# The recurrent mixer's (1 + t)/(1 − t) rewritten with an exponential on ScalarE, silu by Tanh, and a gate buffer with one place for odd and one for even blocks

## The chip, the cores and the metric

The kernel runs on one core of one Trainium2 chip. The metric is the time of one execution on the device in microseconds. A core has a matrix engine (TensorE, PE in the profile), an elementwise engine (VectorE, DVE), an engine for functions by table (ScalarE, ACT), a general engine (GpSimd, POOL), and a queue engine that here issues nearly all DMAs (SyncE, SP). Each runs its own instructions in the order in which they were written for it, and waits for others through semaphores. Matrix products are collected in PSUM, eight banks of 512 float32 columns by 128 partitions.

## The reference, cut to what matters

One decoder layer on x of 1024 tokens by 1024 features: a norm, one wide projection, an attention mixer (compressed, selected and window branches) and a recurrent mixer, each with a silu gate, merged and projected out. The recurrent mixer, which the change rewrites, is

```
uc = conv_b + sum(up[:, k:k + S] * conv_w[k] for k in range(4))
r = sigmoid(uc @ lru_wa + lru_ba);  i = sigmoid(uc @ lru_wx + lru_bx)     # block diagonal
log_a = -8 * r * softplus(-lru_lambda)
a = exp(log_a);  b = sqrt(-expm1(2 * log_a)) * (i * uc)
h[s] = a[s] * h[s - 1] + b[s]
y_b = (h * silu(g_lru)) @ w_proj_b
```

and the compression of keys and values is silu(flat @ w1 + b1) @ w2, whose key part is then normalised by its mean square.

## The kernel before

Float32 products are made of three products of split operands: mm3 (L169 to L172) issues hi·hi, lo·hi and hi·lo, so every product is a group of three matmuls. The hi part of a tile is written by ACT and the lo part by a subtraction on DVE or POOL.

The stage that the change touches is the first quarter of the program, up to some 250 us of it. The recurrent mixer works on 512 channels as four blocks of 128 channels by all 1024 tokens. `lru(n)` is a generator in two parts: first two chunks of the input projection (the convolution's input and the gate g_lru), the convolution and the silu gate; then two gate products of 128x1024 (the gates r and i, into PSUM banks named ps_t, of which there are two), the recurrence's coefficients, and the scan. `compress()` is a generator too. A string sets in which order their parts are written:

```
ORD = "0c1c0c2c1c323"
```

Behind it `qkv` projects all eight token blocks with matmuls of 262 columns into banks ps_s and ps_f; each finished block is copied out by ACT (L510, L511) and twelve gate columns by DVE (L512, bg). `prep` (L533 to L580) then normalises the block's queries and keys in steps that are handed out between other work: ACT squares (L543), DVE sums (L545), POOL takes the root (L192, L193), DVE multiplies (L548), POOL applies the gains (L549, L550), ACT and DVE split into hi and lo (L553 to L558, and POOL L562 for the values), PE transposes (L566, L573) into ps_t, ACT and DVE cast these (L568, L577). The attention's scores begin at L624.

The coefficients before: with t = tanh(half the log of a) the kernel uses a = (1 + t)/(1 − t), and sqrt(1 − a²) = 2 sqrt(−t)/(1 − t). ACT makes t (L368) and sqrt(−t) (L369); DVE 1 − t (L373), its reciprocal (L374), the two products (L375, L376); POOL i·uc (L377), DVE its product with the root (L378), the scan (L379), POOL the product with the gate (L380).

A scheduler places the instructions of each engine in order of a priority that counts up as the program is written; `urgent(by)` lowers it by so much for what is written inside. The kernel has a ring of nine tiles t of 128x1024, and one tile kTs, which here holds the silu gate in its first half and the gate i in its second.

Of the kernel before, what the change touches and what calls it, by code (L numbers as in the profile page):

```python
# [9 lines left out]
FT = mybir.dt.float32  # L10
FR = mybir.dt.float32r
AF = mybir.ActivationFunctionType
# [5 lines left out]
S = 1024  # L18
# [3 lines left out]
HD = 64  # L22
# [48 lines left out]
F_LEAD = 3.13  # L71


def f(ap):
    return ap.bitcast(FT)
# [11 lines left out]
def _build(ctx, tc, A, out, dbg):  # L87
# [217 lines left out]
    with tc.issue_after(last_c), tc.issue_after(last_v):  # L305
        C.activation(gw_h, gw_raw, AF.Copy)
        V.tensor_tensor(out=gw_l, in0=gw_raw, in1=f(gw_h), op=OP.subtract)
        cb1 = part["cb1"].rearrange("p (j h) -> p j h", j=2)
        pe = part["pe"].rearrange("p (j l) -> p j l", j=2)
# [18 lines left out]
        V.tensor_scalar(out=m4sp, in0=y[:, 5], scalar1=-8.0, scalar2=None, op0=OP.mult)  # L328


    yb = DR.tile([4, 128, S], FT, name="yb")

    def lru(n):
# [17 lines left out]
        si = K.tile([128, 2, 64 + S], FT, name="kTs", bufs=1)  # L351
        sg, i = si[:, 0, :S], si[:, 1, :S]
        for half in range(2):
            t = slice(half * 512, (half + 1) * 512)
            C.activation(sg[:, t], s[half], AF.Sigmoid)
            V.tensor_tensor(out=sg[:, t], in0=sg[:, t], in1=s[half], op=OP.mult)
        yield
        r = u
        for w, b_, g_ in ((0, ba, r), (1, bx, i)):
            for half in range(2):  # L360
# [3 lines left out]
                C.activation(g_[:, t], s, AF.Sigmoid, bias=b_[:, n:n + 1])  # L364
        sc = m4sp[:, n:n + 1]

        a, q = ta(), ta()
        C.activation(a, r, AF.Tanh, scale=sc)  # L368
        C.activation(q, a, AF.Sqrt, scale=-1.0)  # L369
        if LE == 2:  # L370
            C.activation(r, a, AF.Copy, scale=-1.0, bias=1.0)
        else:
            EN[LE].tensor_scalar(out=r, in0=a, scalar1=-1.0, scalar2=1.0, op0=OP.mult, op1=OP.add)  # L373
        V.reciprocal(r, r)  # L374
        V.scalar_tensor_tensor(out=a, in0=a, scalar=1.0, in1=r, op0=OP.add, op1=OP.mult)  # L375
        V.scalar_tensor_tensor(out=q, in0=q, scalar=2.0, in1=r, op0=OP.mult, op1=OP.mult)  # L376
        EN[IE].tensor_tensor(out=i, in0=i, in1=uc, op=OP.mult)  # L377
# [7 lines left out]
    def compress():  # L385
# [7 lines left out]
        for j in range(2):  # L393
# [29 lines left out]
            for hf in range(2):  # L423
                z = s[hf][:, 0:128]
                C.activation(sg[:, hf], z, AF.Sigmoid, bias=cb1[:, j, hf:hf + 1])
                V.scalar_tensor_tensor(out=hid[:, hf], in0=z, scalar=cb1[:, j, hf:hf + 1], in1=sg[:, hf],
                                       op0=OP.add, op1=OP.mult)
# [6 lines left out]
            if j == 0:  # L434
# [4 lines left out]
                rsq(ss, ss, HD * EPS, 64, 2)  # L439
# [12 lines left out]
            else:  # L452
                for r in (slice(0, 64), slice(64, 128)):
                    C.activation(vcc[r, :, 0], ov, AF.Copy)
# [664 lines left out]
```

## Time and profile before

| | |
|---|---|
| median of three runs | 905.2 us (902.38 to 905.53) |
| the profiled execution | 903.51 us, span of the trace 901.7 us |
| mean granted clock of TensorE | 0.996 |
| busy share | PE 97%, DVE 63%, ACT 49%, POOL 33% |
| the chain of work that ended last | PE 83%, DVE 6%, POOL 3%, DMA 3%, ACT 3% of the span |

The trace shows one execution. Busy time is the time in which an engine executes, as a share of the span; the chain that ended last is followed back from the last instruction, at each step to what released it. Matmuls are pipelined: one that lasts 0.39 us can be followed by the next 0.23 us after its start, so starts are compared, not durations. A wait is the idle time of an engine just before an instruction, put down to the instruction that released it.

### The profile page before, as it was taken

Reading aid. Unit: us, or ns where it says so; the run is one execution under the profiler, and the core shown is the slowest. Engines: PE = TensorE matmul, PEld = TensorE weight load, DVE = VectorE, ACT = ScalarE, POOL = GpSimd, SP = SyncE. Lnnn points to the kernel's source line nnn. Section 1 sums busy time; section 2 is a strip of 40 time slices with the busy share of each in tenths; the row PEclk is TensorE's granted clock in tenths of the full one; section 3 lists DMA queues with packets and bytes.
Section 4 is the critical chain, followed back from the end, with each engine's and each line's share of the span. In section 5 each row is a group of like instructions: output and inputs, shape, how many; then the busy total and the mean of one; then the engine's idle time right before and its main releaser. Section 6 shows DMA issues by size and latency. Waiting matters only on the chain.

```text
span 901.7 us, 15836 instructions
## 1 busy us (share of the span) xinstructions
PE 872.1 (97%) x5670; PEld 779.5 (86%) x5670; DVE 569.1 (63%) x1627; ACT 441.4 (49%) x1161; POOL 298.5 (33%) x338
## 2 busy tenths in 40 slices
PE   5999999989899999999999999999999999999998
PEld 4778888989899999999999998999998877888887
DVE  4563868897622548576577857667777886783111
ACT  7432453646423547566456757566667663331000
POOL 4032243279512435253355644233324421000000
PEclk9999999999999999999999999999999999999999
DMA  9133421202212112112122241121113369883121
GB/s 354 53 99 114 155 87 48 77 30 76 101 48 83 47 60 84 64 53 77 48 65 77 67 138 54 37 71 56 40 46 117 125 212 342 330 271 109 71 71 47
DMA packets 45519, 92.49 MB, mean 103 GB/s; under 512 B 6896, under 2 KB 12704, under 8 KB 45440
## 3 DMA queue, kind: packets, MB, share of 16 engines
q1 hardware_dynamic: 44480, 88.33, 29.3%
q0 software_dynamic: 960, 3.15, 0.9%
q8 instruction: 44, 0.72, 0.3%
q14 instruction: 35, 0.29, 0.1%
HBM read 64.15 MB, written 25.21 MB: 99 GB/s over the span
## 4 chain that ended last, share of the span: by engine, by line
PE 83%; DVE 6%; POOL 3%; DMA 3%; ACT 3%; issue 1%; SPq 0%; ACTq 0%; DVEq 0%; POOLq 0%
PE ps_f L170 10%; PE ps_f L171 9%; PE ps_f L172 9%; PE ps_s L624 7%; PE ps_s L170 7%; PE ps_s L172 7%; PE ps_s L171 7%; PE ps_t L677 6%; PE ps_t L170 4%; PE ps_t L171 4%; PE ps_t L172 4%; PE ps_o L701 3%; PE ps_o L702 3%; DVE sq L548 1%; POOL ss L193 1%
## 5 line engine op out<-in xcount | busy, mean ns | idle before, releaser
L171 PE MATMUL ps_f<-big_l,w_hi 128*128 128x256 f32 (+1 forms) x700 | 200.3, 286 | 0.0
L170 PE MATMUL ps_f<-big_h,w_hi 128*128 128x256 f32 (+1 forms) x664 | 193.8, 292 | 0.8 <-ACT ev L841 0.6
L172 PE MATMUL ps_f<-big_h,w_lo 128*128 128x256 f32 (+1 forms) x664 | 189.6, 286 | 0.0
L171 PEld LDWEIGHTS ps_f<-big_l,w_hi 128*128 128x128 f32 x700 | 131.9, 188 | 2.0
L170 PEld LDWEIGHTS ps_f<-big_h,w_hi 128*128 128x128 f32 x664 | 125.6, 189 | 4.5 <-ACT ev L841 2.0
L172 PEld LDWEIGHTS ps_f<-big_h,w_lo 128*128 128x128 f32 x664 | 125.4, 189 | 1.8 <-POOL w_lo L185 0.3
L682 DVE TENSOR_TENSOR pl<-ps_t,ph 128x512 fp32r<-128x512 f32 x132 | 90.4, 687 | 47.1 <-ACT ph L681 45.6
L185 POOL TENSOR_TENSOR w_lo<-w_raw,w_hi 128x1024 fp32r<-128x1024 f32 x32 | 77.9, 2438 | 97.6 <-ACT w_hi L184 75.0
L681 ACT ACTIVATE ph<-ps_t 128x512 fp32r<-128x512 f32 x132 | 78.1, 599 | 48.8 <-PE ps_t L677 45.5
L662 POOL TENSOR_SCALAR p_slc<-p_slc,mx,bg 128x384 f32<-128x384 f32 (+7 forms) x88 | 68.6, 785 | 90.1 <-DVE mx L661 35.3
L658 ACT ACTIVATE p_slc<-ps_s,mx 128x256 f32<-128x256 f32 (+5 forms) x128 | 68.1, 540 | 24.0 <-DVE mx L656 18.2
L171 PE MATMUL ps_s<-big_l,w_hi 128*128 128x512 f32 (+1 forms) x184 | 73.2, 398 | 0.0
L184 ACT ACTIVATE w_hi<-w_raw 128x1024 fp32r<-128x1024 f32 (+1 forms) x40 | 42.3, 1061 | 38.3 <-PE ps_f L171 17.7
L648 DVE TENSOR_REDUCE mx<-ps_s 128x1 f32<-128x256 f32 (+5 forms) x120 | 50.9, 436 | 10.7 <-PE ps_s L624 9.2
L701 PE MATMUL ps_o<-ph,t 128*128 128x512 f32 x132 | 55.7, 422 | 0.0
L170 PE MATMUL ps_s<-big_h,w_hi 128*128 128x512 f32 x136 | 54.4, 408 | 0.4 <-ACT big_h L245 0.3
L662 POOL TENSOR_SCALAR p_win<-p_win,mx,bg 128x640 f32<-128x640 f32 (+1 forms) x40 | 34.7, 869 | 59.1 <-DVE mx L661 25.0
L677 PE MATMUL ps_t<-ident_r,p_slc 128*128 128x128 f32 x336 | 54.0, 273 | 0.0
L653 DVE CUSTOM_DVE_ANT_0 ps_s<-ps_s,bias 128x256 f32<-128x256 f32 (+1 forms) x128 | 52.5, 417 | 2.3 <-POOL p_win L662 0.8
L172 PE MATMUL ps_s<-big_h,w_lo 128*128 128x512 f32 x136 | 53.4, 395 | 0.4 <-POOL w_lo L185 0.4
L624 PE MATMUL ps_s<-kTs,t 128*128 128x512 f32 (+4 forms) x224 | 53.0, 349 | 0.3 <-ACT pc L633 0.3
L702 PE MATMUL ps_o<-pl,t 128*128 128x512 f32 x132 | 53.2, 403 | 0.0
(332 smaller groups left out, 2209.9 us busy)
## 6 DMA issues: line engine op xcount, KB each, us to landing
w_raw<-in_w_in SPq DMA_DIRECT2D x30, 512.0 KB
t<-in_x SPq DMA_DIRECT2D x8, 512.0 KB
gb<-ev SPq DMA_DIRECT2D x16, 256.0 KB
ga<-ev SPq DMA_DIRECT2D x16, 256.0 KB
w_raw<-in_w_out SPq DMA_DIRECT2D x8, 512.0 KB
st<-mb SPq DMA_DIRECT2D x16, 256.0 KB
w_raw<-in_w_tok SPq DMA_DIRECT2D x6, 524.0 KB
ev<-in_cw SPq DMA_DIRECT2D x8, 256.0 KB
```

The lines of the kernel that those rows point to most:

```text
L170: T.matmul(o, lh, rh, start=first, stop=False)
L171: T.matmul(o, lh, rl, start=False, stop=False)
L172: T.matmul(o, ll, rh, start=False, stop=last)
L185: (E or (V if tail else G)).tensor_tensor(out=lo, in0=raw, in1=f(hi), op=OP.subtract)
L624: T.matmul(s, qT[h][:, i * 128:(i + 1) * 128], rhs, start=(hl == 0), stop=(hl == 1))
L658: C.activation(p[:, h, k0:k1], sv, AF.Exp, bias=mx[:, 6:7], accum_out=mx[:, 7 + j:8 + j])
L662: G.tensor_scalar(out=p[:, h], in0=p[:, h], scalar1=mx[:, 9:10], scalar2=bg[:, g, i, 4 * (br + 1) + h:4 * (br + 1) + h + 1], op0=OP.mult, ...
L677: ins = T.transpose(pt[:, h * 128:(h + 1) * 128], p[h][:, c0:c0 + 128], ident)
L681: C.activation(ph, pt, AF.Copy)
L682: V.tensor_tensor(out=pl, in0=pt, in1=f(ph), op=OP.subtract)
L701: T.matmul(o, vf, pp[0], start=first, stop=False)
L702: T.matmul(o, vf, pp[1], start=False, stop=False)
```

## The change

Algebra: with a = (1 + t)/(1 − t), 1/(1 − t) is (1 + a)/2. So `r` becomes a by an exponential on ACT (L378 of the changed kernel, with a new column of scales m8sp, twice m4sp), and the two factors are made from it: q = (1 + a)·½sqrt(−t), and a again as (1 + a)·t + 1, which is the old formula written out. The half in q is made good by a gate of twice the silu: (tanh(z/2) + 1)·z. The compression's silu is written in the same way; its keys are normalised with 4 eps, its values halved in the copy out of PSUM. That silu is written under urgent(600). The gate i is computed ahead of r, into a tile of the ring of its own, and the tile kTs is taken once, with one half for the gate of even blocks and one for that of odd blocks. The product i·uc (POOL) is written ahead of the coefficients. The diff:

```diff
--- before.py
+++ after.py
@@ -69,6 +69,7 @@
 F_PREP = 1.24
 F_JOB = 1.16
 F_LEAD = 3.13
+UH = 600
 
 
 def f(ap):
@@ -306,6 +307,8 @@
         C.activation(gw_h, gw_raw, AF.Copy)
         V.tensor_tensor(out=gw_l, in0=gw_raw, in1=f(gw_h), op=OP.subtract)
         cb1 = part["cb1"].rearrange("p (j h) -> p j h", j=2)
+        cb1h = K.tile([128, 2, 2], FT, name="cb1h")
+        V.tensor_scalar(out=cb1h, in0=cb1, scalar1=0.5, scalar2=None, op0=OP.mult)
         pe = part["pe"].rearrange("p (j l) -> p j l", j=2)
 
 
@@ -326,9 +329,13 @@
         V.tensor_tensor(out=y[:, 5], in0=y[:, 5], in1=y[:, 6], op=OP.add)
         m4sp = K.tile([128, 4], FT, name="m4sp")
         V.tensor_scalar(out=m4sp, in0=y[:, 5], scalar1=-8.0, scalar2=None, op0=OP.mult)
+        m8sp = K.tile([128, 4], FT, name="m8sp")
+        V.tensor_scalar(out=m8sp, in0=m4sp, scalar1=2.0, scalar2=None, op0=OP.mult)
 
 
     yb = DR.tile([4, 128, S], FT, name="yb")
+
+    si = K.tile([128, 2, 64 + S], FT, name="kTs", bufs=1)
 
     def lru(n):
         s = chunk(2 * n)
@@ -348,33 +355,31 @@
         C.activation(uh, uc, AF.Copy)
         EN[UE >> n & 1].tensor_tensor(out=ul, in0=uc, in1=f(uh), op=OP.subtract)
         s = chunk(2 * n + 1)
-        si = K.tile([128, 2, 64 + S], FT, name="kTs", bufs=1)
-        sg, i = si[:, 0, :S], si[:, 1, :S]
+        sg, i = si[:, n % 2, :S], ta()
         for half in range(2):
             t = slice(half * 512, (half + 1) * 512)
-            C.activation(sg[:, t], s[half], AF.Sigmoid)
-            V.tensor_tensor(out=sg[:, t], in0=sg[:, t], in1=s[half], op=OP.mult)
+
+            C.activation(sg[:, t], s[half], AF.Tanh, scale=0.5)
+            V.scalar_tensor_tensor(out=sg[:, t], in0=sg[:, t], scalar=1.0, in1=s[half], op0=OP.add, op1=OP.mult)
         yield
         r = u
-        for w, b_, g_ in ((0, ba, r), (1, bx, i)):
+        for w, b_, g_ in ((1, bx, i), (0, ba, r)):
             for half in range(2):
                 s = ps_t()
                 t = slice(half * 512, (half + 1) * 512)
                 mm3(s, gw_h[:, w, n], gw_l[:, w, n], uh[:, t], ul[:, t], True, True)
                 C.activation(g_[:, t], s, AF.Sigmoid, bias=b_[:, n:n + 1])
+        EN[IE].tensor_tensor(out=i, in0=i, in1=uc, op=OP.mult)
         sc = m4sp[:, n:n + 1]
+
 
         a, q = ta(), ta()
         C.activation(a, r, AF.Tanh, scale=sc)
-        C.activation(q, a, AF.Sqrt, scale=-1.0)
-        if LE == 2:
-            C.activation(r, a, AF.Copy, scale=-1.0, bias=1.0)
-        else:
-            EN[LE].tensor_scalar(out=r, in0=a, scalar1=-1.0, scalar2=1.0, op0=OP.mult, op1=OP.add)
-        V.reciprocal(r, r)
-        V.scalar_tensor_tensor(out=a, in0=a, scalar=1.0, in1=r, op0=OP.add, op1=OP.mult)
-        V.scalar_tensor_tensor(out=q, in0=q, scalar=2.0, in1=r, op0=OP.mult, op1=OP.mult)
-        EN[IE].tensor_tensor(out=i, in0=i, in1=uc, op=OP.mult)
+        C.activation(r, r, AF.Exp, scale=m8sp[:, n:n + 1])
+        C.activation(q, a, AF.Sqrt, scale=-0.25)
+        V.scalar_tensor_tensor(out=q, in0=r, scalar=1.0, in1=q, op0=OP.add, op1=OP.mult)
+        V.scalar_tensor_tensor(out=a, in0=r, scalar=1.0, in1=a, op0=OP.add, op1=OP.mult)
+        EN[LE].tensor_scalar(out=a, in0=a, scalar1=1.0, scalar2=None, op0=OP.add)
         EN[JE >> n & 1].tensor_tensor(out=i, in0=i, in1=q, op=OP.mult)
         V.tensor_tensor_scan(out=q, data0=a, data1=i, initial=0.0, op0=OP.mult, op1=OP.add)
         EN[YE >> n & 1].tensor_tensor(out=q, in0=q, in1=sg, op=OP.mult)
@@ -422,9 +427,12 @@
             hid, sg = [hs[:, o:o + 256].rearrange("p (h c) -> p h c", h=2) for o in (0, 256)]
             for hf in range(2):
                 z = s[hf][:, 0:128]
-                C.activation(sg[:, hf], z, AF.Sigmoid, bias=cb1[:, j, hf:hf + 1])
-                V.scalar_tensor_tensor(out=hid[:, hf], in0=z, scalar=cb1[:, j, hf:hf + 1], in1=sg[:, hf],
-                                       op0=OP.add, op1=OP.mult)
+
+                with urgent(UH):
+                    C.activation(sg[:, hf], z, AF.Tanh, scale=0.5, bias=cb1h[:, j, hf:hf + 1])
+                    V.tensor_scalar(out=hid[:, hf], in0=z, scalar1=cb1[:, j, hf:hf + 1], scalar2=None, op0=OP.add)
+                    V.scalar_tensor_tensor(out=hid[:, hf], in0=sg[:, hf], scalar=1.0, in1=hid[:, hf],
+                                           op0=OP.add, op1=OP.mult)
             o = ps_t()
             for g in range(2):
                 for hf in range(2):
@@ -436,7 +444,7 @@
                 ss = hs[0:64, 640:642]
                 for g in range(2):
                     C.activation(kq[:, g], ov[:, g], AF.Square, accum_out=ss[:, g:g + 1])
-                rsq(ss, ss, HD * EPS, 64, 2)
+                rsq(ss, ss, 4 * HD * EPS, 64, 2)
                 V.tensor_tensor(out=kq, in0=ov, in1=ss[:, :, None].to_broadcast([64, 2, 64]), op=OP.mult)
                 V.tensor_tensor(out=kq, in0=kq, in1=kgain[0:64, None, 0, :].to_broadcast([64, 2, 64]), op=OP.mult)
                 st = ta(FR)[0:64, 0:512].rearrange("p (g l a d) -> p g l a d", g=2, l=2, a=2)
@@ -451,8 +459,9 @@
                 C.activation(kcT, pt[:, 0:256].rearrange("p (g l c) -> p g l c", g=2, l=2), AF.Copy)
             else:
                 for r in (slice(0, 64), slice(64, 128)):
-                    C.activation(vcc[r, :, 0], ov, AF.Copy)
-                    V.tensor_tensor(out=vcc[r, :, 1], in0=ov, in1=f(vcc[r, :, 0]), op=OP.subtract)
+                    C.activation(vcc[r, :, 0], ov, AF.Copy, scale=0.5)
+                    V.scalar_tensor_tensor(out=vcc[r, :, 1], in0=ov, scalar=0.5, in1=f(vcc[r, :, 0]),
+                                           op0=OP.mult, op1=OP.subtract)
             yield
 
     parts = {"0": lru(0), "1": lru(1), "2": lru(2), "3": lru(3), "c": compress()}
```

The rows below are each engine's instructions in their order, with the numbers of the tiles; line numbers are those of each kernel.

ACT, from the last gates of block 2 to the first of block 3 (t_862 is r of block 2 and kTs i; t_1099 r of block 3), before:

```order
L364 ACTIVATE t_862<-ps_t_1172,small_73 128x512
L364 ACTIVATE t_862<-ps_t_1177,small_73 128x512
L368 ACTIVATE t_1192<-t_862,m4sp_420 128x1024
L364 ACTIVATE kTs_930<-ps_t_1182,small_73 128x512
L369 ACT_TABLE_LOAD
L369 ACTIVATE t_1193<-t_1192 128x1024
L364 ACT_TABLE_LOAD
L364 ACTIVATE kTs_930<-ps_t_1187,small_73 128x512
L364 ACTIVATE t_1099<-ps_t_1205,small_73 128x512
```

and now (t_937 is i of block 2, t_869 r, t_1176 i of block 3):

```order
L371 ACTIVATE t_937<-ps_t_1186,small_73 128x512
L371 ACTIVATE t_869<-ps_t_1191,small_73 128x512
L371 ACTIVATE t_869<-ps_t_1196,small_73 128x512
L377 ACTIVATE t_1202<-t_869,m4sp_422 128x1024
L378 ACT_TABLE_LOAD
L378 ACTIVATE t_869<-t_869,m8sp_424 128x1024
L379 ACT_TABLE_LOAD
L379 ACTIVATE t_1203<-t_1202 128x1024
L371 ACT_TABLE_LOAD
L371 ACTIVATE t_1176<-ps_t_1214,small_73 128x512
```

The Exp and its table load have come in, and the last sigmoid of block 2 no longer stands between the Tanh and the square root; the first sigmoid of block 3 is behind three loads.

DVE, at the end of block 2 and in block 3 (t_1193 becomes the state of block 2's scan; sq, st and ss belong to the first prep, bias is a table for the attention), before:

```order
L374 RECIPROCAL t_1099<-t_1099 128x1024
L379 SCALAR_TENSOR_TENSOR t_1193<-t_1192,kTs_930 128x1024
L467 COPY bias_1238<-t_1239 128x1024
L548 TENSOR_TENSOR sq_1344<-ev_1340,ss_1346 128x384
L467 COPY bias_1238<-t_1242 128x1024
L512 COPY bg_358<-ps_s_1351 128x12
L545 TENSOR_REDUCE ss_1437<-sq_1435 128x6
```

and now (t_1203 is that state; t_1108, t_1235 and t_1236 are a, t and the root of block 3):

```order
L382 TENSOR_SCALAR t_1202<-t_1202 128x1024
L384 SCALAR_TENSOR_TENSOR t_1203<-t_1202,t_937 128x1024
L557 TENSOR_TENSOR sq_1353<-ev_1349,ss_1355 128x384
L521 COPY bg_358<-ps_s_1360 128x12
L380 SCALAR_TENSOR_TENSOR t_1236<-t_1108,t_1236 128x1024
L381 SCALAR_TENSOR_TENSOR t_1235<-t_1108,t_1235 128x1024
L476 COPY bias_1247<-t_1248 128x1024
L554 TENSOR_REDUCE ss_1446<-sq_1444 128x6
L563 TENSOR_TENSOR st_1376<-sq_1353,st_1376 128x4x64
L383 TENSOR_TENSOR t_1176<-t_1176,t_1236 128x1024
L567 TENSOR_TENSOR st_1379<-sq_1353,st_1379 128x2x128
```

The reciprocal ahead of the scan is gone; two products of block 3 now stand between the copy of the gate columns and the split of the first prep (L563, L567).

PE, around the first prep's transposes (ps_s_1623 and ps_s_1624 are the two banks of the fifth token block, ps_s_1541 and ps_s_1542 of the fourth; st is the split query and key), before at row 893:

```order
L170 MATMUL ps_s_1623<-w_hi_1282,big_h_74 128x262
L566 MATMUL ps_t_1383<-ident_r_66,st_1367 128x128 x4
L573 MATMUL ps_t_1398<-ident_r_66,st_1370 128x128 x4
L171 MATMUL ps_s_1623<-w_lo_1283,big_h_74 128x262
L172 MATMUL ps_s_1623<-w_hi_1282,big_l0_75 128x262
```

and now at row 838:

```order
L173 MATMUL ps_s_1542<-p_slc_1279,big_l1_76 128x262
L575 MATMUL ps_t_1392<-ident_r_66,st_1376 128x128 x4
L582 MATMUL ps_t_1407<-ident_r_66,st_1379 128x128
L171 MATMUL ps_s_1541<-p_slc_1279,big_h_74 128x262
L172 MATMUL ps_s_1541<-p_slc_1279,big_h_74 128x262
```

The transposes have moved forward by 55 rows, from within the fifth token block into the end of the fourth.

## Rows read from the trace of the kernel before

**Rows 1.** The page: busy time, share of the span and instructions of each engine.

```profile
PE 872.1 (97%) x5670; PEld 779.5 (86%) x5670; DVE 569.1 (63%) x1627; ACT 441.4 (49%) x1161; POOL 298.5 (33%) x338
```

**Rows 2.** Windows: stretch; busy PE, PEld, DVE, ACT, POOL; clock, DMA, GB/s.

```profile
102.00:160.00 58.00, 57.46 (x288) 46.41 (x288) 46.76 (x39) 21.55 (x35) 19.69 (x10) 1.00 0.24 81
...
176.00:190.00 14.00, 11.08 (x89) 10.66 (x88) 14.00 (x9) 5.65 (x15) 6.50 (x6) 1.00 0.38 111
190.00:235.00 45.00, 40.96 (x325) 39.90 (x326) 37.44 (x67) 22.23 (x71) 41.26 (x47) 0.96 0.22 75
235.00:250.00 15.00, 15.00 (x114) 15.00 (x114) 7.26 (x32) 8.34 (x26) 4.52 (x6) 0.90 0.17 63
```

**Rows 3.** Waits of PE, 160 to 260: waiter, releaser, total us, times, longest.

```profile
PE ps_s L170 <- DVE bg L512: 2.8, 1, 2.8
PE ps_s L624 <- ACT t L577: 2.4, 1, 2.4
```

**Rows 4.** Timeline of PE: start, us, line, operation; idle time before in brackets.

```profile
160.23 0.39 PE L170 MATMUL ps_t<-t,bias 128*128 128x512 f32 x1
...
189.89 0.39 PE L170 MATMUL ps_s<-w_hi,big_h 128*128 128x262 f32 x1 [2.80 <-DVE bg L512]
...
194.07 0.28 PE L170 MATMUL ps_s<-p_slc,big_h 128*128 128x262 f32 x1
194.19 0.29 PE L171 MATMUL ps_s<-p_slc,big_h 128*128 128x262 f32 x1
```

**Rows 5.** Lines of DVE, 90 to 205: count, busy us, mean ns, idle before.

```profile
L374 DVE RECIPROCAL t<-t 128x1024 f32<-128x1024 f32 x4 | 26.2, 6550 | 0.1
...
L376 DVE SCALAR_TENSOR_TENSOR t<-t 128x1024 f32<-128x1024 f32 x4 | 5.4, 1348 | 0.0
L373 DVE TENSOR_SCALAR t<-t 128x1024 f32<-128x1024 f32 x4 | 2.8, 690 | 7.7 <-ACT t L368 7.7
```

**Rows 6.** Timeline of DVE, 176 to 206.

```profile
183.60 2.22 DVE L379 TENSOR_TENSOR_SCAN t<-t,kTs 128x1024 f32<-128x1024 f32 x1
...
186.33 2.71 DVE L548 TENSOR_TENSOR sq<-ev,ss 128x384 f32<-128x384 f32 x1
...
194.83 2.55 DVE L554 TENSOR_TENSOR st<-sq,st 128x256 fp32r<-128x256 f32 x1
...
197.38 0.41 DVE L558 TENSOR_TENSOR st<-sq,st 128x256 fp32r<-128x256 f32 x1
...
200.15 0.55 DVE L548 TENSOR_TENSOR sq<-ev,ss 128x384 f32<-128x384 f32 x1
```

**Rows 7.** Lines of ACT, 90 to 205, columns as in group 5.

```profile
L364 ACT ACTIVATE kTs<-ps_t,small 128x512 f32<-128x512 f32 x8 | 5.4, 690 | 2.7 <-PE ps_t L172 2.7
...
L368 ACT ACTIVATE t<-t,m4sp 128x1024 f32<-128x1024 f32 x4 | 4.6, 1148 | 0.1
```

**Rows 8.** Timeline of ACT, 94 to 174.

```profile
97.49 1.28 ACT L369 ACT_TABLE_LOAD   x1
98.78 1.06 ACT L369 ACTIVATE t<-t 128x1024 f32<-128x1024 f32 x1
...
170.61 0.39 ACT L510 ACTIVATE ev<-ps_f 128x262 f32<-128x262 f32 x1
...
171.80 0.37 ACT L511 ACTIVATE ev<-ps_s 128x250 f32<-128x250 f32 x1
...
173.10 0.52 ACT L543 ACTIVATE sq<-ev 128x384 f32<-128x384 f32 x1
```

**Rows 9.** Timeline of POOL, 176 to 236.

```profile
185.95 2.66 POOL L380 TENSOR_TENSOR t<-t,kTs 128x1024 f32<-128x1024 f32 x1 [7.24 <-issue]
...
190.91 1.71 POOL L549 TENSOR_TENSOR sq<-sq,small 128x256 f32<-128x256 f32 x1
...
194.68 2.42 POOL L377 TENSOR_TENSOR kTs<-kTs,t 128x1024 f32<-128x1024 f32 x1
...
208.25 0.74 POOL L549 TENSOR_TENSOR sq<-sq,small 128x256 f32<-128x256 f32 x1 [0.50 <-DVE sq L548]
```

## The prediction

> **What bounds the kernel now.** I read the page's busy times first: TensorE (PE) is busy 97% of the span and VectorE (DVE), from which the change takes work, 63% [rows 1]. So the sum can only be made from the few stretches in which PE idles, and the table of windows shows them [rows 2]: PE is full from 102 to 160 but for 0.54 us, and full again from 235 on; between 176 and 235 it is idle for (14 − 11.08) + (45 − 40.96) = 7.0 us. The waits of PE say for whom [rows 3]: 2.8 us for a DVE copy of gate columns (L512) that empties a PSUM bank, 2.4 us for an ACT cast at the end of the last preparation of a token block; the rest are short waits for DVE. The timeline of PE [rows 4] shows the first: a matmul starts at 189.89 after 2.80 us idle. After each of the two the granted clock falls to the lower of its levels of 1.2 and 2.4 GHz for a while: a mean of 0.96 over the 45 us is 3.6 us at half clock, 1.8 lost, and 0.90 over the next 15 is 3.0 us, 1.5 lost [rows 2]. I take 1.5 for each, since the first mean is rounded. In all the trace holds 0.5 + 7.0 + 3.0 = 10.5 us that a better fed PE could win, and nothing else in reach.
>
> Why PE waits at 187 is in the timeline of DVE [rows 6]: the last block's reciprocal, 6.55 us [rows 5], fills DVE until 183.6, the scan of the block before it comes behind, then a product L548 that takes 2.71 us where an undisturbed one takes 0.55, and only then the copy for which PE waits. L548 is long because POOL multiplies 128x1024 elements at the same time [rows 9]; POOL itself stood for 7.24 us, since that product needs the scan, and the gains of the first token block's preparation are queued behind it. POOL is then busy 41.26 of 45 us [rows 2]: the second long wait, near 234, is the tail of a chain of preparations that began 7 us late. So one cause, the reciprocal in DVE's queue, stands ahead of both.
>
> **What the change removes.** Per recurrent block a reciprocal of 6.55 us and the subtraction of 0.69; it adds a+1 with the form of that subtraction (0.69 taken, since it is the same operation on the same tile). Net −6.55 by four blocks, −26.2 us of DVE [rows 5]. Off the path this is worth nothing; its value is the 10.5 us above, less what the edit makes PE wait anew.
>
> **What it adds.** Exp is no row of the trace; its nearest is Tanh with a scale from a tile, 1.15 us [rows 7], the same shape (Sqrt, 1.06 [rows 8], is the lower bound). Four of them are 4.6 us. The order shows 16 table loads instead of 13, three more of 1.28 us: Exp and Sqrt each have a load of their own, and the next sigmoid needs a third, where a block had two; loads at the silu of before go. ACT is busy 49%, so 8.5 us more are hidden in sum; they are not hidden where PE's next gate tile waits for ACT. Silu through Tanh has the shape of silu through Sigmoid: 0. Compression gets four DVE additions of 128 columns out of PSUM, each at most L373's 0.69 us for 1024 [rows 5]; in the new order PE comes to the product that reads them some 23 matmuls of 512 columns later, 23 x 0.238 = 5 us, so they are covered and the 0.54 us wait between 102 and 160 goes; without that cover two of them could make it 1.9 us.
>
> **Where PE waits anew.** I followed the new order with these durations.
> (a) The last block's gates. The r gate's first PSUM bank is the one that i's first half frees, and that sigmoid now stands in ACT's queue behind block 2's whole chain: sigmoid 0.69, Tanh 1.15, load 1.28, Exp 1.15, load 1.28, Sqrt 1.06, load 1.28, sigmoid 0.69 = 8.58 us [rows 7, 8]. From block 2's last r matmul to the last block's first, PE has 50 matmuls of 262 columns and 6 of 512. One of 262 takes 0.122, start to start [rows 4], one of 512 by its columns 0.238: 7.5 us. Wait: 1.1 us. Bounds: 0.7, if the four functions overlap by 0.1 each, to 2.4, if the evictions of 0.39 and 0.37 and the square of 0.52 [rows 8] fall inside. It uses up the 0.9 us that PE has gained till then (the 0.54 us and a little of block 1). The same count for blocks 0 and 1 leaves PE a margin of 0.7 and 0.8 us; I take 0.
> (b) The first preparation's transposes (L575, L582). They move forward by 55 rows of PE's queue, into the token tile ahead. PE's times are counted from its first gate matmul of block 2, at 160.23 [rows 4], less the 0.9 us of lead: 18 matmuls of 512 and 78 of 262 columns, 13.8 us, to the wait of (a), its 1.1, then six and two, 1.7, to the last gate product (175.9), then 94 by 0.122: PE is there at 187.4. The halves that it transposes come from DVE L563 and L567, queued behind products of the last block that wait for its Sqrt. That Sqrt ends 0.2 + 0.69 + 1.15 + 1.28 + 1.15 + 1.28 + 1.06 = 6.8 us after PE's last gate (0.2 for the matmul's own end), at 182.7, or 1.3 later if the evictions and the square of (a) fall between. DVE then has, in its order, 3 x 1.35 for products of the block (L376's form), 0.69 for a copy of the same tile, 0.55 for a reduction of 384 columns, and 2 x 0.41 for L563 and L567 [rows 5, 6]: 6.1, of which I take off 0.5 since starts overlap their predecessors a little (the scan's end, 185.82, lies before 186.33 by less than the copy between them). So L567 is through at 188.3 to 189.6, where PE, after the transposes of the first half, would be at 187.8: 0.5 to 1.8 us, and 2.5 if POOL's gain operations stretch a copy or a product by 0.7. I take 1.5. All the remaining token tiles stand behind it in PE's queue, so it is paid in full. What is late here is ACT's chain, no longer the reciprocal.
> (c) The second preparation's transposes. PE has 51 matmuls more to them and the rest of the first transposes, 6.6 us, and comes at about 195.5. Their split stands behind the last scan on DVE (2.2), and POOL's product with the gate starts as that scan ends; beside such a product the split took 2.55 us instead of 0.41 [rows 6]. From 188.3 to 189.6 on the queue holds a+1 (0.69), the scan, copies and reductions (1.5), the normalising product (0.55) and the splits (0.8): 194.0 to 195.3 with nothing stretched, up to 198.5 with one split and half of another operation stretched. So 0 to 3.0 us, and up to 1.5 for the clock; I take 2.0, between the ends, since rows 6 show the one split stretched and the other not.
> (d) The other preparations. In the new order PE has about 36 matmuls of 262 columns and two groups of transposes of 0.3 between them: 36 x 0.122 + 0.6 = 5.0 us. POOL's work for one of the seven that fall into its 41.26 us is (41.26 − 3 x 2.4)/7 = 4.9 us, with the three 128x1024 operations that lie in the stretch taken out [rows 2, 9]. They keep pace; I take 0.4. The first scores (L624) come 6 us after their casts, since the chain begins near 183 and not behind the product that ends at 188.6 [rows 9]: the 2.4 us go, with the clock behind them. With that cover gone they would stay, and 3.9 of the 10.5 with them.
> DMAs: the store of the gated product moves with it by a few us and is read only in the output stage; on SP's queue the loads behind it are those of before, and of block 3's store only six small loads of a bias table change sides with it, so 0.
>
> **Sum.** 1.1 + 1.5 + 2.0 + 0.4 = 5.0 of new waits, against 10.5 won: −5.5 us on the profiled execution, whose span of 901.7 and 1.8 us around it are 903.5. The median of before is 905.2, 1.7 above it, so I put the same difference there: 905.2 − 5.5 = 899.7. A measurement can tell about 0.5%, 4.5 us, since three runs of before spread by 0.35%: faster means below 900.7. The forecast stands 1 us beyond that border.
>
> **Rivals.**
> R1, the wait moves on. (c) at 3.0 + 1.5 and (b) at 2.5, with the rest as above: 1.1 + 2.5 + 4.5 + 0.4 = 8.5, gain 2.0, time 903.2. For it: L548 and L554 are stretched beside POOL products in rows 6, and the order still puts the same product of POOL beside the same work. Against: the product now starts before PE is near.
> R2, the change doesn't do what it says: the idle time is that of POOL's preparations (busy 41.26 of 45), and the reciprocal only hid beside them. Gain 0 to 1, time 904.7. Against: POOL stood 7.24 us for the scan behind that reciprocal.
> R3, the new waits stay at their lower ends, 0.7 + 0.5 + 0 + 0 = 1.2: gain 9.3, time 895.9.
> R4, the other side: PE's queue asks for each preparation every 5.0 us, and POOL can't keep it. If the three 128x1024 operations stay in the stretch, a preparation costs 41.26/7 = 5.9 us instead of 4.9; and L549 takes 0.74 or 1.71 us [rows 9], which would add 0.5 if half of those that are short now were long: 6.4. Six more gaps of 1.4 are 8.4 us, and with a clock loss of 3 and the 5.0 above 16.4 are lost against 10.5 won: 911. It decides from a cadence of about 6.2 us, where 6 x 1.2 + 5.0 + 3 pass 15. Against: in this order the big products are done by about 200.
> R5, slower too: ACT pauses around each table load. The trace has a load at 97.49 of 1.28 us and the Sqrt at 98.78, no gap [rows 8]. Were there a pause as long again as the load, the three loads in (a) would make its wait 3.8 longer and block 1, less its margin of 0.8, lose 3.0; with 1.5 for the clock at each, 9.8 more are lost: 909.5. The Trainium skill's page "ScalarE: Activation LUTs", section "What ACT_TABLE_LOAD costs", has such a pause: a drain of about 1.38 us beside the 1.28 of the load. By that rule (3 x 1.38 in place of 3 x 1.28) the change would lose, an estimate of 910; the rows show no drain.
>
> **Chances.** Forecast 0.45; R1 0.30; R2 0.07; R3 0.08; R4 0.07; R5 0.03. Taken evenly over 897 to 902, the forecast lies below 900.7 in three quarters: 0.33; R3 adds 0.08, and the part of R1 with the smaller waits 0.07: faster 0.48. Slower is R4, R5 and 0.03 of R1 with more stretched splits: 0.13. Same is the rest, 0.39. The range, 895 to 906, takes in the forecast, R1, R2 and most of R3, with the bounds of (a) to (c); R4, R5 and the tails stay out, under 2 in 10.
>
> **What would show it.** Right: no reciprocal of 128x1024 on DVE and its busy time near 545; ACT's near 450; the slow clock gone near 190 and 235; a wait of PE of about 1 us for a gate sigmoid (ACT L371) near 175; POOL at the first preparation's gains by 184; PE 5 us earlier than before at all that follows 250. Wrong: a wait of over 3 us at L575, L582 or a PSUM bank between 186 and 235 (R1, R4); POOL busy over 6 us per preparation (R4); gaps between a table load and the function behind it (R5).

## The result, and the profile after

The changed kernel takes 0.9928 of the time before, 95% interval 0.9909 to 0.9948 (median of its executions at full clock 896.51 against 902.93 us), and in a second set of runs 0.9944, 0.9930 to 0.9958 (899.23 against 903.93). The forecast, 899.7 against 905.2, is 0.9939: gained are 5 to 6.5 us where 5.5 were expected. The rows below are of an execution of 897.41 us, span 895.6, at a mean granted clock of 0.996; two other profiled executions, one of 1001.85 us at a granted clock of 0.805 and one of 4838.86 us, are left out.

The page of the changed kernel, busy times (for [rows 1]):

```profile
PE 869.8 (97%) x5670; PEld 779.8 (87%) x5670; DVE 539.9 (60%) x1629; ACT 450.3 (50%) x1168; POOL 298.9 (33%) x338
```

DVE has lost 29.2 us (26.2 expected) and ACT has 8.9 more (8.5 expected). Its windows, columns as in [rows 2]:

```profile
102.00:160.00 58.00, 58.00 (x296) 47.56 (x296) 37.49 (x39) 28.82 (x41) 17.38 (x9) 1.00 0.25 83
160.00:176.00 16.00, 14.32 (x100) 13.21 (x99) 5.89 (x7) 14.72 (x18) 2.60 (x2) 1.00 0.11 34
176.00:190.00 14.00, 12.54 (x100) 12.20 (x98) 12.68 (x12) 10.58 (x20) 13.34 (x9) 1.00 0.44 130
190.00:235.00 45.00, 42.72 (x348) 42.31 (x349) 32.00 (x77) 24.85 (x80) 34.06 (x43) 0.96 0.22 67
235.00:250.00 15.00, 15.00 (x124) 15.00 (x123) 5.45 (x21) 5.17 (x16) 5.27 (x8) 1.00 0.23 88
...
200.00:205.00 5.00, 5.00 (x31) 5.00 (x31) 4.49 (x7) 1.99 (x9) 4.92 (x7) 0.66 0.26 107
```

PE is full up to 160; from there to 235 it is idle for 1.68 + 1.46 + 2.28 = 5.4 us, where before it was 7.0, and of the two stretches at half clock one is left, at 200 to 205 (5 us at 0.66 are 3.4 at half clock, 1.7 lost). Nearly all of the idle time is in three waits of PE, 100 to 250 us (for [rows 3]):

```profile
PE ps_t L575 <- DVE t L577: 1.9, 1, 1.9
PE ps_t L575 <- DVE st L563: 1.8, 1, 1.8
PE ps_t L171 <- ACT t L371: 1.7, 1, 1.7
```

and the timeline of PE says where they stand:

```profile
175.19 0.50 PE L171 MATMUL ps_t<-t,bias 128*128 128x512 f32 x1 [1.68 <-ACT t L371]
...
190.33 0.54 PE L575 MATMUL ps_t<-ident_r,st 128*128 128x128 f32 x4 [1.79 <-DVE st L563]
...
199.69 0.54 PE L575 MATMUL ps_t<-ident_r,st 128*128 128x128 f32 x4 [1.89 <-DVE t L577]
...
240.80 0.38 PE L686 MATMUL ps_t<-ident_r,p_win 128*128 128x128 f32 x2
```

These are the places (a), (b) and (c) of the prediction. At (a) and (b) the releaser is the instruction that it named; at (c) it is on the engine named, DVE, but is another instruction. DVE's timeline there:

```profile
195.61 2.58 DVE L384 TENSOR_TENSOR_SCAN t<-t 128x1024 f32<-128x1024 f32 x1
...
198.30 0.42 DVE L563 TENSOR_TENSOR st<-sq,st 128x256 fp32r<-128x256 f32 x1
...
199.34 0.29 DVE L577 CAST t<-ps_t 128x128 fp32r<-128x128 f32 x1
```

The split of the second preparation (L563) is done at 198.72. PE waits on until the last cast of the first preparation's transposes (L577) has emptied the bank, at 199.63. Both stand behind the last scan.

The last row of PE's timeline is the first window transpose: before it started at 245.56, so PE leads by 4.8 us there. The spans differ by 6.1; the rest comes behind 250 us, where no term of the prediction lies, and executions of the kernel before alone spread from 901.46 to 905.53.

ACT's timeline ahead of the first of these waits, with the three loads (for [rows 7, 8]):

```profile
168.33 1.28 ACT L378 ACT_TABLE_LOAD   x1
169.63 1.15 ACT L378 ACTIVATE t<-t,m8sp 128x1024 f32<-128x1024 f32 x1
170.78 1.28 ACT L379 ACT_TABLE_LOAD   x1
172.08 1.06 ACT L379 ACTIVATE t<-t 128x1024 f32<-128x1024 f32 x1
173.16 1.28 ACT L371 ACT_TABLE_LOAD   x1
174.45 1.27 ACT L371 ACTIVATE t<-ps_t,small 128x512 f32<-128x512 f32 x2
```

Each function starts 0.01 to 0.02 us after its load; Exp takes 1.15, as taken from Tanh.

So far the time and the places of the waits are as forecast. But the prediction said why, too: that one cause, the reciprocal, stood ahead of both long waits. The experiments took that apart.

### The profile page after: what moved, and what is told of

Read it like the earlier page. It is cut to its first block, busy times and chain, and to the rows that moved or that the text cites. A ratio compares the mean times of both kernels' runs of the same rounds, so it can differ in the third digit from the quotient of the medians.

```text
span 1000.1 us, 15845 instructions
## 1 busy us (share of the span) xinstructions
PE 982.1 (98%) x5670; PEld 854.5 (85%) x5670; DVE 537.8 (54%) x1629; ACT 454.2 (45%) x1168; POOL 296.6 (30%) x338
## 4 chain that ended last, share of the span: by engine, by line
PE 93%; POOL 2%; ACT 2%; DVE 1%; issue 1%; DMA 1%; SPq 0%; ACTq 0%; DVEq 0%; POOLq 0%
PE ps_f L172 10%; PE ps_f L173 10%; PE ps_f L171 10%; PE ps_s L171 9%; PE ps_s L172 9%; PE ps_s L173 9%; PE ps_s L633 8%; PE ps_t L686 7%; PE ps_t L171 4%; PE ps_t L173 4%; PE ps_t L172 4%; PE ps_o L711 3%; PE ps_o L710 3%; PE ps_s L422 1%; PE ps_t L244 1%
## 5 line engine op out<-in xcount | busy, mean ns | idle before, releaser
L172 PE MATMUL ps_f<-big_l,w_hi 128*128 128x256 f32 (+1 forms) x700 | 214.2, 306 | 0.0
L171 PE MATMUL ps_f<-big_h,w_hi 128*128 128x256 f32 (+1 forms) x664 | 207.9, 313 | 0.1
L173 PE MATMUL ps_f<-big_h,w_lo 128*128 128x256 f32 (+1 forms) x664 | 204.1, 307 | 0.0
L172 PEld LDWEIGHTS ps_f<-big_l,w_hi 128*128 128x128 f32 x700 | 142.1, 203 | 3.5
L171 PEld LDWEIGHTS ps_f<-big_h,w_hi 128*128 128x128 f32 x664 | 134.6, 203 | 4.8 <-ACT t L344 1.0
L173 PEld LDWEIGHTS ps_f<-big_h,w_lo 128*128 128x128 f32 x664 | 134.5, 203 | 2.6
L172 PE MATMUL ps_s<-big_l,w_hi 128*128 128x512 f32 (+1 forms) x184 | 83.9, 456 | 0.0
L171 PE MATMUL ps_s<-big_h,w_hi 128*128 128x512 f32 x136 | 62.7, 469 | 0.3 <-ACT big_h L246 0.3
L173 PE MATMUL ps_s<-big_h,w_lo 128*128 128x512 f32 x136 | 61.4, 454 | 0.0
L686 PE MATMUL ps_t<-ident_r,p_slc 128*128 128x128 f32 x336 | 60.8, 299 | 0.0
```

The source lines that it names most:

```text
L171: T.matmul(o, lh, rh, start=first, stop=False)
L172: T.matmul(o, lh, rl, start=False, stop=False)
L173: T.matmul(o, ll, rh, start=False, stop=last)
L686: ins = T.transpose(pt[:, h * 128:(h + 1) * 128], p[h][:, c0:c0 + 128], ident)
```

## The experiments

Each ratio is to the kernel before on the same chip, with its 95% interval.

**The change once more**, first timed and then for its trace.

> The changed kernel as it is, for a trace at full clock. Theory (the prediction's account): 0.993 of before; PE idles 3 to 5 us between 160 and 235 in three new places, about 1 us for a gate sigmoid of block 3 (ACT L371), about 1.5 at the first preparation's transposes (L575 or L582, for DVE L563 or L567), about 2 at the second's; no long stretch at half clock near 190 and 235. Rival (the new waits do not come, R3): the same time, but PE idle under 1.5 us in 160 to 235 and all of the 10.5 us won.

> The changed kernel once more, for a trace at full clock. As before: by the prediction's account PE idles 3 to 5 us in 160 to 235, at a gate sigmoid of block 3 and at the first two preparations' transposes; by R3 under 1.5 us. The kernel with all but the algebra left 5.3 us there without a half-clock stretch, so a third reading is that the change too keeps about 3 to 4 us of short waits, none long enough for the clock to fall.

Measured: 0.9944, and the trace shown above: 5.4 us idle in three waits, a little more than the 3 to 5 expected, and one stretch at half clock. R3 is out.

**The algebra alone.** The kernel before, with

```diff
-        C.activation(q, a, AF.Sqrt, scale=-1.0)
-        EN[LE].tensor_scalar(out=r, in0=a, scalar1=-1.0, scalar2=1.0, ...)
-        V.reciprocal(r, r)
+        C.activation(r, r, AF.Exp, scale=m8sp[:, n:n + 1])
+        C.activation(q, a, AF.Sqrt, scale=-1.0)
...
```

> The kernel before with only the coefficients rewritten (Exp, two products, a + 1; Sqrt without the factor a quarter since the gate stays a plain silu): r ahead of i, silu by Sigmoid and the one gate buffer as before. Theory (the reciprocal in DVE's queue is the cause): most of the gain, 0.993 to 0.997 of before, the rest lost to a fourth table load per block, since Exp, a sigmoid, Sqrt and a sigmoid follow each other on ACT. Rival A (the order of gates, the gate buffer and the Tanh are what helps, and the reciprocal lay hidden): 0.999 to 1.002. Rival B (table loads on the path): slower than before, 1.003 or more.

Measured: 1.0076, 1.0063 to 1.0090, slower by 7 us, in the range of rival B. My theory falls: the reciprocal is gone and the kernel loses. Its trace, PE and then DVE and ACT:

```profile
111.73 0.33 PE L430 MATMUL ps_t<-t 128*64 128x64 f32 x2 [3.91 <-DVE t L425]
```

```profile
102.52 1.22 DVE L373 SCALAR_TENSOR_TENSOR t<-t 128x1024 f32<-128x1024 f32 x1 [2.72 <-ACT t L372]
...
107.90 1.21 DVE L377 TENSOR_TENSOR kTs<-kTs,t 128x1024 f32<-128x1024 f32 x1
109.03 0.68 DVE L375 TENSOR_SCALAR t<-t 128x1024 f32<-128x1024 f32 x1
...
111.36 0.58 DVE L425 SCALAR_TENSOR_TENSOR t<-ps_s,small,t 128x128 f32<-128x128 f32 x2
```

```profile
116.61 0.60 ACT L357 ACTIVATE kTs<-ps_s 128x512 f32<-128x512 f32 x1 [11.61 <-POOL t L379]
```

PE waits 3.91 us here and 3.55 in the second half of the compression, for the compression's silu (L425). In DVE's queue this silu stands behind the block's products, and these now all wait for the Sqrt at the end of ACT's chain; before, of the block's work only 1 − t and the reciprocal stood ahead of it, which need the Tanh alone. And the last row shows something that I had not weighed at all: ACT's next operation is the silu of the next block's gate, and it stands 11.61 us for POOL's last product of this block, because both use the one tile kTs. The trace has 20 table loads, a fourth in each block, where the kernel before has 13; what rival B makes of that is taken up below, with the gate's place.

**All but the algebra.** The changed kernel with the reciprocal put back.

> The changed kernel with the reciprocal put back (1 - t, reciprocal, the two products of before; no Exp): i ahead of r, Tanh silu, gate buffer by odd and even blocks as in the change. Theory: no gain, 0.998 to 1.003 of before, with waits of 2 us or more for DVE behind the last reciprocal near 187. Rival A: the gain stays, 0.992 to 0.995.

Measured: 0.9961, 0.9947 to 0.9974: between the theory and rival A, with more than half of the gain. Windows of its trace:

```profile
176.00:190.00 14.00, 13.60 (x107) 13.30 (x107) 13.40 (x11) 8.83 (x16) 7.70 (x7) 1.00 0.23 76
190.00:235.00 45.00, 40.66 (x326) 38.72 (x326) 35.79 (x61) 22.53 (x71) 37.34 (x41) 1.00 0.28 89
```

DVE is nearly as full as before (13.40 of 14), and yet PE's long wait at 187 is gone, and the clock doesn't fall. From 190 to 235 PE idles 4.34 us, as before (4.04), but in waits of at most 1.6 us. So the reciprocal was not enough to make the long wait.

**Parts of the change undone or made alone.** Three kernels:

```diff
sigmoid_in_compress, from the changed kernel:
-  C.activation(sg[:, hf], z, AF.Tanh, scale=0.5, bias=cb1h[:, j, hf:hf + 1])
-  V.tensor_scalar(out=hid[:, hf], in0=z, ...)
-  V.scalar_tensor_tensor(out=hid[:, hf], in0=sg[:, hf], scalar=1.0, in1=hid[:, hf], ...)
+  C.activation(sg[:, hf], z, AF.Sigmoid, bias=cb1[:, j, hf:hf + 1])
+  V.scalar_tensor_tensor(out=hid[:, hf], in0=z, scalar=cb1[:, j, hf:hf + 1], in1=sg[:, hf], ...)
...  (the factors 4 of eps and 0.5 of the values are taken out too)
r_before_i, from the changed kernel:
-        for w, b_, g_ in ((1, bx, i), (0, ba, r)):
+        for w, b_, g_ in ((0, ba, r), (1, bx, i)):
i_first_alone, from the kernel before:
-        sg, i = si[:, 0, :S], si[:, 1, :S]
+        sg, i = si[:, 0, :S], ta()
-        for w, b_, g_ in ((0, ba, r), (1, bx, i)):
+        for w, b_, g_ in ((1, bx, i), (0, ba, r)):
```

> The changed kernel with the compression's silu as before (Sigmoid, one product, no halving). Theory 2 (the algebra alone lost because ACT's longer chain held the compression's silu, two PE waits of 3.9 and 3.6 us; the Tanh form is what avoids it): those waits come back, 0.999 to 1.004 of before. Rival (the gates' order alone avoids it): 0.993 to 0.996, no PE wait over 1 us at the compression's second product.

> The changed kernel with r computed ahead of i as before, i still in its own tile. Theory 3 (the order of the gates is what makes Exp cheap: with r first Tanh and Exp start before i's sigmoids, which need their table again, a fourth load per block): 0.998 to 1.005 of before, with PE waits for a gate sigmoid of 1 to 3 us. Rival (order of gates is indifferent): 0.993 to 0.996.

> The kernel before with only i ahead of r and i in a tile of the ring: reciprocal, Sigmoid silu and the rest as before. Theory 3: it spares the wait of a table load between i's halves and puts the chain behind the last sigmoid; of the 3.7 us that all but the algebra won it brings most, 0.995 to 0.998. Rival (the Tanh forms or the gate's two places bring it): 0.999 to 1.002.

Measured: 0.9930 (0.9915 to 0.9944), 0.9937 (0.9924 to 0.9950) and 1.0078 (1.0058 to 1.0099). Theories 2 and 3 fall: the first two kernels come out in the range of the rival, so the Tanh in the compression and the order of the gates are worth nothing in the changed kernel. The third came out where neither its theory nor its rival had it: i ahead of r, with i in a tile of the ring, costs the kernel before 7 us, with waits like those of the algebra alone (timeline of PE):

```profile
147.31 0.47 PE L431 MATMUL ps_t<-t 128*64 128x64 f32 x2 [3.33 <-DVE t L426]
```

With urgent(0) in place of urgent(600) the program comes out the same, so that edit does nothing. What was left is the gate's tile. The kernel before has it in its trace, ACT and DVE, in rows that I had passed over:

```profile
150.95 1.09 ACT L355 ACTIVATE kTs<-ps_s 128x512 f32<-128x512 f32 x2 [4.41 <-POOL t L380]
...
188.65 1.09 ACT L355 ACTIVATE kTs<-ps_s 128x512 f32<-128x512 f32 x2 [0.36 <-POOL t L380]
```

```profile
193.63 1.27 DVE L356 TENSOR_TENSOR kTs<-kTs,ps_s 128x512 f32<-128x512 f32 x2
```

The gate silu of block n + 1 waits for block n's product with the gate on POOL, which in turn waits for the scan. Block 3's is at 188.65, and its two PSUM banks, two of the four named ps_s, come free with DVE's second step behind 193.63. In the changed kernel's trace the same silu runs at

```profile
161.45 0.58 ACT L362 ACTIVATE kTs<-ps_s 128x512 f32<-128x512 f32 x1
```

**The gate's place**, undone in the changed kernel, made alone in the kernel before, and made there with the algebra:

```diff
one_gate_place, from the changed kernel:
-    si = K.tile([128, 2, 64 + S], FT, name="kTs", bufs=1)
...
-        sg, i = si[:, n % 2, :S], ta()
+        si = K.tile([128, 2, 64 + S], FT, name="kTs", bufs=1)
+        sg, i = si[:, 0, :S], ta()
two_places_alone, from the kernel before:
+    si = K.tile([128, 2, 64 + S], FT, name="kTs", bufs=1)
...
-        si = K.tile([128, 2, 64 + S], FT, name="kTs", bufs=1)
-        sg, i = si[:, 0, :S], si[:, 1, :S]
+        sg, i = si[:, n % 2, :S], ta()
two_places_and_algebra: the same, and the diff of the algebra alone
```

> The changed kernel with the gate's tile taken anew by each block, in one place, as before (i keeps its own tile). Theory 4 (with one place the gate silu of block n + 1 has to wait on ACT for POOL's product of block n, and holds two of the four ps_s banks and ACT's queue meanwhile; the two places undo that, and this is what the other edits needed): most of the gain is lost, 0.998 to 1.008 of before, with idle time of ACT of several us ahead of a gate silu for POOL L385. Rival (the gate's place is indifferent): 0.992 to 0.996.

> The kernel before with only the gate's two places, and for that i in a tile of the ring; r first, Sigmoid, reciprocal as before. Theory 4: 0.994 to 0.998, as all but the algebra had. Rival (taking i out of the gate's tile costs by itself, as i first alone lost 7 us): 1.002 to 1.010.

> The kernel before with the gate's two places, i in its own tile, and the coefficients by Exp; r first and both silus by Sigmoid as before. Theory 4: these two are the whole of the change's gain, 0.992 to 0.995. Rival (Tanh for the gate silu is needed, since Sigmoid and Tanh forms differ in table loads or in what DVE does): 0.997 or more.

Measured: 0.9971 (0.9960 to 0.9982), 1.0006 (0.9996 to 1.0016) and 0.9924 (0.9912 to 0.9936). The first lies between its theory and its rival: with one place the changed kernel keeps about half of its gain. In it, ACT idles 9.56 and 8.81 us for POOL ahead of the gate silus of blocks 1 and 2, and at the place of the old 2.80 us wait [rows 4] PE waits longer, in PE's timeline and DVE's:

```profile
192.61 0.39 PE L171 MATMUL ps_s<-w_hi,big_h 128*128 128x262 f32 x1 [4.26 <-DVE kTs L362]
```

```profile
191.88 0.67 DVE L362 SCALAR_TENSOR_TENSOR kTs<-kTs,ps_s 128x512 f32<-128x512 f32 x1
```

The releaser is the gate silu's second step, and the bank that PE wants is the one that it empties: the hold is shown. The second run missed its theory and its rival: the two places alone are worth nothing. PE waits elsewhere, at the late preparations and at evictions (waits of PE, 160 to 260):

```profile
PE ps_t L574 <- DVE t L578: 4.9, 2, 2.7
PE ps_s L170 <- ACT ev L511: 2.6, 1, 2.6
```

And with the reciprocal the two places don't free ACT either, in POOL's timeline and ACT's of this run:

```profile
120.64 2.40 POOL L381 TENSOR_TENSOR t<-t,kTs 128x1024 f32<-128x1024 f32 x1 [3.48 <-DVE t L380]
```

```profile
123.07 0.60 ACT L356 ACTIVATE kTs<-ps_s 128x512 f32<-128x512 f32 x1 [7.72 <-POOL t L381]
```

The gate silu of block 2 stands 7.72 us for POOL's product of block 0, which reads the same half of the tile. With Exp in the place of the reciprocal (the third kernel) that product starts at 113.70, and the silu, at 121.06, has no wait for it. This is one way in which the two edits need each other; how much of the 7 us it makes is not shown.

The third hit: both together, with r first and Sigmoid everywhere, have all of the change's gain. It also bears on rival B of the algebra alone. ACT's square root of block 0, there and here:

```profile
101.43 1.06 ACT L372 ACTIVATE t<-t 128x1024 f32<-128x1024 f32 x1
```

```profile
103.78 1.06 ACT L373 ACTIVATE t<-t 128x1024 f32<-128x1024 f32 x1
```

Here, with 16 loads in the program and not 20, the root ends 2.35 us later, and PE has no wait for the compression's silu. So a late end of ACT's chain doesn't make that wait by itself; DVE's order does its part, for here the silu stands ahead of a + 1 and of the product with i·uc. What the fourth load costs by itself no run separates.

**POOL relieved.** The two waits left at the first preparations' transposes, taken on. IE = 1 and YE = 15 in the changed kernel put i·uc and the product with the gate on DVE.

> The changed kernel with i times uc and the state times the gate on DVE for all blocks (1.2 us each there, 2.4 to 3.1 on POOL). Theory (the two waits at the first preparations' transposes, 1.8 and 1.9 us, are POOL's queue and DVE operations stretched beside POOL's products): both shrink under 1 us in sum, the gate sigmoid's 1.7 stays, 0.989 to 0.992 of before. Rival (DVE's queue ahead of the splits is the limit, and gets 2.4 us longer): 0.994 to 0.998.

Measured: 0.9911, 0.9898 to 0.9924, the lowest so far, 1.5 to 3 us below the changed kernel; the intervals overlap. Waits of PE, 90 to 300:

```profile
PE ps_t L171 <- ACT t L371: 1.3, 1, 1.3
PE ps_s L171 <- ACT ev L519: 1.3, 1, 1.3
PE ps_t L575 <- DVE t L577: 0.8, 1, 0.8
PE ps_t L575 <- DVE st L563: 0.6, 1, 0.6
```

The two at L575 shrink from 3.7 to 1.4 us, a little over the 1 expected, and new ones stand beside them, 1.3 us for an eviction and 0.5 at L582. From 190 to 235 the granted clock is 1.00, where it was 0.96, so the 1.7 us of (c)'s slow stretch are won as well. So POOL's products made most of (b) and (c).

**A spare bank.** In the same kernel, `s = ps_o() if (n, w, half) == (3, 0, 0) else ps_t()` for the gates.

> The kernel of the run before (i times uc and state times gate on DVE), and the first half of block 3's r gate in the spare PSUM bank ps_o instead of a bank that i's sigmoid has to free. Theory (that wait of PE, 1.3 us there and 1.7 in the changed kernel, is for a PSUM bank held behind ACT's chain of three table loads): it goes, 0.988 to 0.990 of before, 1 to 1.5 us less than without the bank. Rival (ACT's chain is late for the next thing as well, and the wait comes back at another bank, at an eviction or at the first preparation): 0.990 to 0.993, the same as without.

Measured: 0.9902, 0.9886 to 0.9919, medians of 896.13 and 895.68: no difference that can be told. The rival holds. Waits of PE:

```profile
PE ps_t L575 <- DVE st L563: 2.1, 2, 1.2
PE ps_s L171 <- ACT ev L519: 1.4, 1, 1.4
PE ps_t L171 <- ACT t L371: 1.3, 1, 1.3
```

The wait of 1.3 us is at the next gate tile, and more has come at L575: ACT's chain is late for what comes next, whichever bank is first.

## Why the prediction was right, point by point

- **What PE could win**, 10.5 us in four places: both long waits are gone, the 0.54 us ahead of 160 and one of the two slow stretches too.
- **The new waits.** (a) 1.1 forecast, 1.68 measured, for the sigmoid named. (b) 1.5 and 1.79. (c) 2.0 and 1.89, with the clock behind it, which I had put into the 2.0: 1.7 us more lost; and its last releaser was the cast that empties the bank, not the split. (d) nothing, 0.4 forecast. In sum 5.4 us idle and 1.7 of clock, 7.1, against 5.0.
- **Luck in the sum.** By these terms only 10.5 − 7.1 = 3.4 us are won. But the 897 matmuls up to the first window transpose that run from 100.38 to 245.56 before run from 100.92 to 240.80 now, in 139.9 us instead of 145.2, 5.3 less. Of the 1.9 us between, 0.4 is clock: windows of 5 us give the kernel before 0.66 at 190, 0.97 at 230 and 0.69 at 235, 3.4 us lost and not 3.0. The rest lies in stretches in which PE counts as busy, and its cause stays open. So the new waits were 2.1 us larger than forecast, a gain that no term held made up for nearly as much, and the time came out right partly by luck.
- **Why (b) is late** was only half right. I had its DVE steps wait for the last Sqrt, at 182.7 to 184.0; it ended at 184.5. But DVE came to the first product only at 185.73, because of POOL, which came to the first gains at 185.81 and not by 184 (changed kernel, POOL's timeline and DVE's):

```profile
175.79 3.13 POOL L372 TENSOR_TENSOR t<-t 128x1024 f32<-128x1024 f32 x1 [8.67 <-ACT t L371]
...
179.63 3.31 POOL L194 TENSOR_TENSOR ss<-ss,nhalf 128x6 f32<-128x6 f32 x1
182.91 2.40 POOL L385 TENSOR_TENSOR t<-t,kTs 128x1024 f32<-128x1024 f32 x1
185.81 1.74 POOL L558 TENSOR_TENSOR sq<-sq,small 128x256 f32<-128x256 f32 x1 [0.50 <-DVE bg L521]
```

```profile
177.33 2.15 DVE L382 TENSOR_SCALAR t<-t 128x1024 f32<-128x1024 f32 x1
179.51 2.29 DVE L384 TENSOR_TENSOR_SCAN t<-t 128x1024 f32<-128x1024 f32 x1
...
182.98 2.75 DVE L557 TENSOR_TENSOR sq<-ev,ss 128x384 f32<-128x384 f32 x1 [1.18 <-POOL ss L194]
```

  L194, 1.3 us undisturbed, takes 3.31 beside DVE's scan, L557 waits for it and then lies beside POOL's product at 182.91 for 2.75 us instead of 0.55. With these products on DVE (POOL relieved) the wait is 0.6: L194 takes 3.31 there too, but L557 only 0.56.
- **The step that failed** is the sentence that one cause, the reciprocal in DVE's queue, stands ahead of both long waits. The kernels at the four corners say otherwise: with one gate place and the reciprocal 1; with Exp in its place and no other edit 1.0076; with two places (and i in a tile of the ring) and the reciprocal 1.0006; with both 0.9924. Made in the kernel before, neither part alone gains, and one loses; together they gain 7 us. Undone in the changed kernel, each leaves about half of the gain or a little more (0.9971 with one place, 0.9961 with the reciprocal). The reciprocal made DVE late, and the single gate tile made ACT, and two of the four ps_s banks, wait for POOL at the end of each block; the 4.26 us wait with one place shows that hold. It is not shown that the hold makes the algebra alone lose: 7.5 us of PE's waits there are for the compression's silu, and the changed kernel with one place, which has Exp too, has no wait at that product. I had the change's third part in the order (the gate's place) and gave it no term, since its wait, 0.36 us in ACT's row, looked small; what it held, the banks, is in no wait of ACT's.
- **Small sizes.** a + 1 was taken at 0.69 us; here it takes 1.65 on average, 2.15 beside POOL's product in block 2, so DVE's relief is not where the forecast put it. The clock fell behind the wait of 1.89 us and not behind that of 1.79.
- **The rivals.** R1 is excluded by its time, 903.2, and not by its waits: (c) with its clock cost 3.6 us, between the 2.0 forecast and R1's 4.5, and the 7.1 us in all lie nearer to R1's 8.5 than to 5.0. R2 (the reciprocal only hid) is refuted for the change as a whole: with two gate places Exp takes the time from 1.0006 to 0.9924. R4: POOL was busy 34.06 of 45 us where it had been 41.26 [rows 2], so its cadence kept up. R5: no pause at the three loads shown above, for the functions start 0.01 to 0.02 us behind them. The Trainium skill's page "ScalarE: Activation LUTs", section "What ACT_TABLE_LOAD costs", has a drain of about 1.38 us beside the 1.28 of the load. These rows don't bear it out.

Open: why the kernel with all but the algebra (0.9961) beats that with the two places alone (1.0006), when i first and the Tanh forms are worth nothing beside Exp. Each edit also moves the order that the scheduler makes. The compression's second product in its first half stands at row 424 of PE's order in the three kernels with one place and Sigmoid gates; PE waits for it 0.54 us in the kernel before, 3.91 with the algebra alone and 1.93 with i first. It stands at row 446 in the changed kernel with one place and at rows 435 to 464 in those with two places, and PE has no wait there. So the row goes along with the wait, whatever the number of gate places; that it decides is argued, not shown.

## What to carry to other kernels

When an operation is taken out of a queue, look for what its waiting neighbours hold: a tile with one place, used by a late product on another engine, keeps PSUM banks and an in-order queue shut for as long, and such a hold can show as the idle time of an engine that nobody is waiting for by name. Two edits of which neither gains alone can gain together, so make the corners (each alone, both, none) before giving a cause. Check the terms of a sum as well as its total, for errors in two of them can cancel, as here. And an operation that waits for the end of a longer chain of functions should not have a small, urgent one behind it in its queue.

## What the runs showed of the hardware that I had not expected

Operations of DVE and POOL stretched beside each other. On DVE, a + 1 on 128x1024 took 0.69 us in block 0 and 2.15 in block 2, beside a POOL product of 3.13; it ended 0.56 us behind that product. DVE's product on 128x384 took 0.55 us undisturbed and 2.75 beside a POOL product of 2.40, and ended 0.42 behind it. POOL's operation on 128x6 took 3.31 us beside DVE's scan, where others of its kind took 1.3, and ended 1.14 behind it. So each of the three ended about when it would have, had it begun at the other's end.

The granted clock stayed at its full level, 2.4 GHz, after PE had idled 1.79 us (until 190.33), and fell to half for about 3.4 us after the next long idle time, of 1.89 us (until 199.69). With the algebra alone it fell after an idle time of 1.56 us (until 203.85; 0.66 from 205 to 210). So the length of the last idle time alone doesn't tell whether it falls.
